# First scale row in two quarters of 256 columns; the first three up-projections over two of eight contraction tiles at once

## The chip, the cores and the metric

One core of one Trainium2 chip runs the whole layer as one program. The metric is the device time in microseconds (us) of one execution; a run gives several executions, and the median counts. A profiled execution also has a span, from its first to its last instruction, which is a little shorter than its device time.

## The reference, cut to what matters

The layer is a half-step gated feed-forward (SwiGLU), a pair of attention mixers, and a second half-step feed-forward. Only the way into the first feed-forward is touched:

```python
m = jnp.split((jax.nn.silu(c) @ w_ada[l] + b_ada[l])[:, None, :], N_MOD, axis=-1)     # 9 rows of 1024
x = _residual(x, _swiglu(_modnorm(x, g[0], m[0], m[1]), w1, w3, w2), g[1], m[2], HALF_STEP)
def _modnorm(x, g_pre, shift, scale):
    return _rmsnorm(x, g_pre) * (1 + scale) + shift
def _swiglu(h, w1, w3, w2):
    return (jax.nn.silu(h @ w1) * (h @ w3)) @ w2
```

`x` is 1024 tokens by 1024 channels, `w1` and `w3` are 1024 by 2816. So before the first product of a token with `w1` there must be the token's norm, and row `m[1]`, the scale, which is itself a product of `silu(c)` with 1024 columns of `w_ada`.

## The kernel before

Products in float32 quality are made of three in a faster format: each operand is split into a high part (ScalarE, a cast) and a low part (VectorE, the difference), and `mm3` adds high·high, high·low and low·high. The big products follow a Strassen scheme: tokens and channels are halved, and a `Unit` (line 500 on) is one tile of 128 output channels. Its `first` multiplies four contraction tiles of 128 channels (k = 0 to 3) of the first 512 tokens with the weight's quarter "11", 12 products of 128x512; its `second` does the same with k = 4 to 7 and "21".

At the head of the program four token tiles (`head`) are loaded, normalised (`normal`, line 910: a square with sum on ScalarE, two small operations on GpSimd, one multiplication on VectorE, in place), and turned by TensorE, so that channels lie on partitions. The turned tile k holds 512 tokens in one bank of PSUM. ScalarE then writes its high part, multiplied by the scale column `a0[:, 0, k]`, and VectorE its low part (`scaled_high`, line 974). ScalarE writes it once more in full (`scaled_all`). The shift row is added later, so the first four units (`RAW`) begin without it.

The scale row is made by `AdaHalf` (line 298), 512 columns at a time. For each of eight k it multiplies `sc[:, k, :]` (silu of c, padded to 32 columns) with 512 columns of `w_ada` in four groups of 128 columns; each group writes its own 32 partitions of one bank. `copy` brings the bank to SBUF, `turn` turns it into columns of 128, and adds the bias; `half_scale` makes `a0` from it. The first half (k = 0 to 3) is made here, two k after each token tile; the second half is made inside the plan.

Up to line 1000 the order of work is the order of the code, on each engine by itself: an engine takes its instructions strictly as they were written, and SyncE (SP) issues every load and store in one queue. From line 1060 a hand-written `Plan` sets the order: `step` lists the main work of TensorE, `side(i, ...)` what other work stands behind step i. Its first steps are `first` of units 0, 1, 2 (in two pieces, with k = 0 and k = 1 to 3) and the `second` of units 0 and 1. Behind step 0 stand the turning of k = 4 to 6, behind step 1 the products of the second row half (`row.step`), its copy and the turning of k = 7, behind step 2 the `half_scale(1)`, so that the row's `turn` comes between the two pieces of unit 2. The flag `units1[0].apart` makes unit 0 take all products that need a low part of the tokens last.

PSUM banks come from three rings, "s" and "m" with three banks, "v" with two; wide SBUF tiles for `w_ada` come from a pool of 16 (`V`).

## Time and profile before

| what | value |
|---|---|
| device time, three runs | 2557.73, 2560.17, 2561.82 us (median 2560.17) |
| device time of the profiled execution | 2559.68 us |
| its span | 2557.7 us |
| TensorE busy | 2527.3 us, 99% of the span |
| VectorE busy | 1936.3 us, 76% |
| ScalarE busy | 1259.2 us, 49% |
| mean of the clock granted to TensorE | 0.998 |
| first matrix instruction, first up-projection product | 9.90 us, 18.80 us |

In the rows of the timeline the columns are: start, length (both us), engine, line, operation, what it writes from what it reads, shape, number of instructions that the row merges, and in brackets the idle time of the engine before it and what ended it. Nearly all operations are recorded by a helper (line 120, 154 or 157), so the tiles' names tell what they are: `bs`, `bm`, `bv` are PSUM banks of the three rings, `sc` the silu of c, `ident` the matrix for turning, `a` the scale column. A row of windows gives, after the stretch and its length, the busy time and the number of instructions of TensorE, its weight loads, VectorE, ScalarE and GpSimd, and then the granted clock, the share of the DMA engines and GB/s. An instruction that reaches into a stretch counts in it.

### The profile page before, as it was taken

Reading aid. Unit: us, or ns where it says so; the run is one execution under the profiler, and the core shown is the slowest. Engines: PE = TensorE matmul, PEld = TensorE weight load, DVE = VectorE, ACT = ScalarE, POOL = GpSimd, SP = SyncE. Lnnn points to the kernel's source line nnn. Section 1 sums busy time; section 2 is a strip of 40 time slices with the busy share of each in tenths; the row PEclk is TensorE's granted clock in tenths of the full one; section 3 lists DMA queues with packets and bytes.
Section 4 is the critical chain, followed back from the end, with each engine's and each line's share of the span. In section 5 each row is a group of like instructions: output and inputs, shape, how many; then the busy total and the mean of one; then the engine's idle time right before and its main releaser. Section 6 shows DMA issues by size and latency. Waiting matters only on the chain. (4 is left out here: it accounts for less than half of the span.)

```text
span 2557.7 us, 38230 instructions
## 1 busy us (share of the span) xinstructions
PE 2527.3 (99%) x13416; PEld 2158.7 (84%) x13416; DVE 1936.3 (76%) x3629; ACT 1259.2 (49%) x2375; POOL 217.8 (9%) x372
## 2 busy tenths in 40 slices
PE   8999999999999999999999999999999999999998
PEld 6888888888998888889888999998888888888887
DVE  4789986887786577874568988887886888767777
ACT  5632223445654653433447987783266322233444
POOL 1000000001000000001003522221011000000003
PEclk9999999999999999999999999999999999999999
DMA  8455543943674666755978733207836445326724
GB/s 307 157 173 195 195 151 117 345 137 132 231 274 138 215 230 225 241 184 176 301 280 275 241 94 76 65 11 262 296 123 216 156 157 169 111 99 233 273 70 165
DMA packets 245760, 479.47 MB, mean 187 GB/s; under 512 B 30464, under 2 KB 71616, under 8 KB 245568
## 3 DMA queue, kind: packets, MB, share of 16 engines
q1 hardware_dynamic: 245568, 477.02, 55.4%
q8 instruction: 106, 1.74, 0.3%
q14 instruction: 86, 0.70, 0.1%
HBM read 348.93 MB, written 127.99 MB: 186 GB/s over the span
## 5 line engine op out<-in xcount | busy, mean ns | idle before, releaser
L120 ACT CAST xu<-t 128x512 fp32r<-128x512 f32 (+1 forms) x270 | 161.0, 601 | 494.4 <-DVE t L120 352.6
L154 PE MATMUL bm<-xu,xu 128*128 128x512 f32 (+2 forms) x1572 | 366.6, 386 | 0.0
L154 PE MATMUL bs<-xv,xu 128*128 128x512 f32 x1488 | 357.3, 389 | 0.3 <-DVE t L120 0.3
L154 PEld LDWEIGHTS bm<-xu,xu 128*128 128x128 f32 x1572 | 288.1, 188 | 56.7
L154 PE MATMUL bv<-xv,xu 128*128 128x512 f32 x1342 | 335.4, 389 | 0.0
L154 PEld LDWEIGHTS bs<-xv,xu 128*128 128x128 f32 x1488 | 279.1, 188 | 59.0 <-issue 1.1
L154 PEld LDWEIGHTS bv<-xv,xu 128*128 128x128 f32 x1342 | 251.8, 188 | 52.3
L154 PE MATMUL bs<-xv,xv 128*128 128x512 f32 x1086 | 265.8, 390 | 0.0
L120 DVE TENSOR_TENSOR xu<-xu,xu 128x512 fp32r<-128x512 f32 (+1 forms) x296 | 201.7, 686 | 55.2 <-ACT xu L120 54.9
L154 PEld LDWEIGHTS bs<-xv,xv 128*128 128x128 f32 x1086 | 203.0, 188 | 41.7
L154 PE MATMUL bs<-xu,xu 128*128 128x512 f32 (+1 forms) x972 | 226.2, 382 | 0.0
L120 DVE TENSOR_TENSOR t<-t,t 128x512 f32<-128x512 f32 (+2 forms) x278 | 185.1, 673 | 45.0 <-ACT t L120 36.0
L154 PE MATMUL bs<-w,w 96*128 96x512 f32 (+3 forms) x832 | 206.5, 367 | 4.7 <-DVE st L1802 4.0
L154 PEld LDWEIGHTS bs<-xu,xu 128*128 128x128 f32 x972 | 177.4, 188 | 35.7 <-issue 1.4
L120 POOL TENSOR_SCALAR st<-st 128x1 f32<-128x1 f32 (+1 forms) x66 | 33.5, 508 | 1887.4 <-ACT t L120 1869.2
L120 ACT CAST xv<-t 128x512 fp32r<-128x512 f32 x170 | 105.8, 622 | 169.8 <-PE bv L154 69.0
L120 DVE TENSOR_TENSOR xu<-t,xu 128x512 fp32r<-128x512 f32 (+1 forms) x270 | 179.0, 663 | 10.7 <-ACT xu L120 10.6
L154 PE MATMUL bm<-xv,xv 128*128 128x512 f32 x690 | 182.8, 390 | 0.0
L120 ACT CAST xu<-xu 128x512 fp32r<-128x512 f32 x218 | 132.7, 618 | 71.3 <-DMA xu<-in_wo 43.6
L120 DVE TENSOR_TENSOR xv<-t,xv 128x512 fp32r<-128x512 f32 x170 | 116.6, 686 | 65.6 <-ACT xv L120 56.5
L154 PE MATMUL bv<-t,w 128*128 128x256 f32 x896 | 150.9, 288 | 2.0 <-DVE t L1940 1.5
L154 PEld LDWEIGHTS bm<-xv,xv 128*128 128x128 f32 x690 | 129.2, 188 | 27.1 <-issue 0.4
(242 smaller groups left out, 4229.3 us busy)
## 6 DMA issues: line engine op xcount, KB each, us to landing
d<-t SPq DMA_DIRECT2D x366, 256.0 KB, 2.6
t<-d SPq DMA_DIRECT2D x274, 256.0 KB, 3.8
xu<-in_f1w SPq DMA_DIRECT2D x59, 512.0 KB, 4.2
xu<-in_f2w SPq DMA_DIRECT2D x58, 512.0 KB, 3.7
t<-in_wada SPq DMA_DIRECT2D x112, 256.0 KB, 5.1
xv<-in_f1w SPq DMA_DIRECT2D x44, 512.0 KB, 7.4
xu<-in_winT SPq DMA_DIRECT2D x38, 512.0 KB, 4.8
w<-d SPq DMA_DIRECT2D x32, 512.0 KB, 6.4
```

Of the source, the lines that this page charges most:

```text
L120: return lambda *x, **y: pin(f(*x, **y))
L154: return pin(nc.tensor.matmul(o, s, m, start=start, stop=stop, skip_group_check=open_group[0]))
```

## The change

The scale's first 512 columns become two quarters of 256 (`AdaQuarter`), each loaded by two transfers of 512 KB in place of four half-tiles' eight of 256 KB. A quarter uses two groups of 128 columns in place of four, and covers two contraction tiles. The first quarter stands ahead of the first up-projection weights in SP's queue, the second behind them. Each token tile is turned for k = 0, 1 only; the first quarter's products stand behind token tiles 1 and 2, its copy before the norm of token tile 3. Tiles k = 2, 3 are turned after that; `first` of units 0, 1 and 2 is called with k = 0, 1, with the second quarter between units 1 and 2, and the plan's main steps keep k = 2, 3 of them. The bank of turned tile 3 comes from ring "v" in place of "m".

```diff
+    class AdaQuarter(AdaHalf):
...
+        def load(self):
+            c = self.m * D + self.q * 256
+            for j in range(2):
+                t = V().rearrange("p (k c) -> p k c", k=4)
+                ld(t, a["wada"][j * 512:(j + 1) * 512, c:c + 256].rearrange("(k p) c -> p k c", p=P))
+                self.r += [t[:, k, :] for k in range(4)]
...
+        def step(self, ks):
+            if self.bank is None:
+                self.bank = PB("v")
+            for k in ks:
+                for g in range(2):
+                    mmul(self.bank[32 * g:32 * g + 32, :P], sc[:, k, :], self.r[k][:, g * P:(g + 1) * P],
+                         start=(k == 0), stop=(k == KD - 1))
...
+    quarters = [AdaQuarter(1, q) for q in range(2)]
...
-    h1rows[0][0].load()
+    quarters[0].load()
     for i in range(3):
         load_halves(i, 0)
+    quarters[1].load()
     h1rows[0][1].load()
...
-    first = [PB(t) for t in "sssm"]
+    first = [PB(t) for t in "sssv"]
     for i, x in enumerate(head):
         normal(x)
-        for k in range(4):
+        for k in range(2):
             turn_(first[k][:, i * P:(i + 1) * P], x[:, k * P:(k + 1) * P], ident)
-        h1rows[0][0].step(range(2 * i, 2 * i + 2))
-    h1rows[0][0].copy()
-    units1[0].split("11")
+        if i in (1, 2):
+            quarters[0].step(range(4 * i - 4, 4 * i))
+        if i == 2:
+            quarters[0].copy()
...
-    half_scale(0)
+    quarter_scale(0)
...
-    for k in range(4):
+    units1[0].cast("11")
+    for k in range(2):
         scaled_high(k, first[k])
+    units1[0].low("11")
+    for k in range(2, 4):
+        for i, x in enumerate(head):
+            turn_(first[k][:, i * P:(i + 1) * P], x[:, k * P:(k + 1) * P], ident)
     units1[1].split("11")
-    for k in range(4):
+    units1[0].first(Raw.f, range(0, 2))
+    units1[1].first(Raw.f, range(0, 2))
+    quarters[1].step(range(KD))
+    quarters[1].copy()
+    units1[2].split("11")
+    quarter_scale(1)
+    for k in range(2):
+        scaled_all(k, first[k])
+    for k in range(2, 4):
+        scaled_high(k, first[k])
+    units1[2].first(Raw.f, range(0, 2))
+    for k in range(2, 4):
         scaled_all(k, first[k])
...
-    go[2:3] = [lambda ks=ks: units1[2].first(Raw.f, ks) for ks in (range(0, 1), range(1, 4))]
+    go[:3] = [lambda u=u, ks=ks: u.first(Raw.f, ks) for u, ks in zip(units1[:3] + units1[2:3], [range(2, 4)] * 2 + [range(2, 3), range(3, 4)])]
```

VectorE at the head, before (rows in the engine's order; `xv_81` to `xv_84` are the four token tiles, `bv` the row's bank, `xu` the weights of a unit):

```order
L120 TENSOR_SCALAR xv_83<-xv_83,st_271 128x1024
L120 TENSOR_SCALAR xv_84<-xv_84,st_290 128x1024
L120 COPY t_306<-bv_240 128x128
L120 TENSOR_TENSOR xu_308<-xu_202,xu_308 128x512
L120 TENSOR_TENSOR mod_103<-bv_312,bada 128x4
L120 SCALAR_TENSOR_TENSOR a_311<-mod_103,ng 128x4
```

The same place with the change:

```order
L120 TENSOR_SCALAR xv_83<-xv_83,st_255 128x1024
L120 COPY t_269<-bv_243 64x128
L120 TENSOR_SCALAR xv_84<-xv_84,st_274 128x1024
L120 TENSOR_TENSOR mod_103<-bv_243,bada 128x2
L120 SCALAR_TENSOR_TENSOR a_280<-mod_103,ng 128x2
...
L120 SCALAR_TENSOR_TENSOR xv_294<-bs_221,a_280,xv_292 128x512
L120 SCALAR_TENSOR_TENSOR xv_294<-bs_222,a_280,xv_292 128x512
L120 TENSOR_TENSOR xu_290<-xu_194,xu_290 128x512
L120 TENSOR_TENSOR xu_309<-xu_196,xu_309 128x512
L120 COPY t_343<-bv_326 64x128
```

The copy of the row moved ahead of the norm of the last token tile (`xv_84`), and the low part of unit 0's weights (`xu_308` before, `xu_290` now) from ahead of the scale's sums to behind the low parts of two token tiles.

TensorE from unit 0's products on, with the change (`xv_292` and `xv_294` are the high and low parts of k = 0, 1; `xv_293` and `xv_295` those of k = 2, 3; `bm_312`, `bm_319`, `bm_359` the banks of units 0, 1, 2); before, all 12 products of unit 0 stood together behind one turning of the row:

```order
L154 MATMUL bm_312<-xv_292,xu_290 128x512
L154 MATMUL bm_312<-xv_294,xu_290 128x512
L154 MATMUL bm_312<-xv_292,xu_290 128x512 x2
...
L154 MATMUL bv_326<-xv_200,sc 32x128 x8
L154 MATMUL bv_326<-xv_202,sc 32x128 x8
L157 MATMUL bv_326<-ident,t_343 128x64
L154 MATMUL bm_359<-xv_292,xu_345 128x512
...
L154 MATMUL bm_312<-xv_293,xu_290 128x512 x4
L154 MATMUL bm_312<-xv_295,xu_290 128x512 x2
L157 MATMUL bs_424<-ident,xv_81 128x128
```

Unit 0's k = 0, 1 now go in plain `mm3` order, where the second product reads the tokens' low part and the third the weights' low part, since the call stands ahead of the line that sets `apart`.

TensorE around the turning of the second row half, before and then with the change (`t_486` and `t_496` are that row's copy, `xv_506` and `xv_515` the high parts of k = 4, 5):

```order
L154 MATMUL bm_496<-xv_322,xu_404 128x512
L157 MATMUL bv_500<-ident,t_486 128x128
L154 MATMUL bm_496<-xv_322,xu_404 128x512
L154 MATMUL bm_496<-xv_324,xu_404 128x512
...
L154 MATMUL bm_496<-xv_323,xu_404 128x512
L154 MATMUL bm_388<-xv_506,xu_422 128x512
```

```order
L154 MATMUL bm_359<-xv_293,xu_345 128x512
L157 MATMUL bv_509<-ident,t_496 128x128
L154 MATMUL bm_359<-xv_293,xu_345 128x512
L154 MATMUL bm_359<-xv_295,xu_345 128x512
L154 MATMUL bm_359<-xv_293,xu_345 128x512
L154 MATMUL bm_312<-xv_515,xu_439 128x512
```

Between the turning and the first product with k = 4 stood nine products of unit 2 before; three stand there now.

More of the change, by code (lines that the diff above doesn't have):

```diff
@@ L328, in turn, with __init__, copy @@
             b = slice(4 * self.h, 4 * self.h + 4)
+            for v in range(2):
+                vec.tensor_tensor(mod[self.m][:, v, b], pv[:, :, v], bada[:, self.m, b], op=ALU.add)
+                yield v
+    class AdaQuarter(AdaHalf):
+        def __init__(self, m, q):
+            self.m, self.q, self.r = m, q, []
+            self.bank = None
+        def load(self):
[11 more added lines that the diff above has]
+                         start=(k == 0), stop=(k == KD - 1))
+        def copy(self):
+            self.rows = T2()
+            vec.tensor_copy(self.rows[0:64, :P], self.bank[0:64, :P])
+        def turn(self):
+            pt = self.bank[:, 256:320]
+            turn_(pt, self.rows[0:64, :P], ident[0:64, 0:64])
+            pv = pt.rearrange("p (g c) -> p g c", c=32)
+            b = slice(2 * self.q, 2 * self.q + 2)
             for v in range(2):
@@ L943, in hybrid_block, with part_scale, quarter_scale @@
     units1[3].load(0)
-    first = [PB(t) for t in "sssm"]
+    first = [PB(t) for t in "sssv"]
     for i, x in enumerate(head):
         normal(x)
-        for k in range(4):
+        for k in range(2):
             turn_(first[k][:, i * P:(i + 1) * P], x[:, k * P:(k + 1) * P], ident)
-        h1rows[0][0].step(range(2 * i, 2 * i + 2))
-    h1rows[0][0].copy()
-    units1[0].split("11")
+        if i in (1, 2):
+            quarters[0].step(range(4 * i - 4, 4 * i))
+        if i == 2:
+            quarters[0].copy()
     banks[0] = "ss"
     a0 = const("a0", [P, 2, KD])
+    def part_scale(row, b):
+        for v in row.turn():
+            vec.scalar_tensor_tensor(a0[:, v, b], mod[1][:, v, b], 1.0, ng[:, 0, b], op0=ALU.add, op1=ALU.mult)
     def half_scale(h):
-        b = slice(4 * h, 4 * h + 4)
-        for v in h1rows[0][h].turn():
-            vec.scalar_tensor_tensor(a0[:, v, b], mod[1][:, v, b], 1.0, ng[:, 0, b], op0=ALU.add, op1=ALU.mult)
-    half_scale(0)
+        part_scale(h1rows[0][h], slice(4 * h, 4 * h + 4))
+    def quarter_scale(q):
+        part_scale(quarters[q], slice(2 * q, 2 * q + 2))
+    quarter_scale(0)
     class Raw:
@@ L1074, in hybrid_block @@
     row, sh = h1rows[0][1], h1rows[1]
-    side(0, lambda: units1[2].split("11"), *[lambda k=k: turn_k(k) for k in range(4, 7)],
+    side(0, *[lambda k=k: turn_k(k) for k in range(4, 7)],
          lambda: units1[0].split("21"), lambda: sh[0].load())
```

## The prediction

> **What bounds the kernel now.** I read the page first, then windows of the whole program, then the timeline of the head.

> ```profile
> PE 2527.3 (99%) x13416; PEld 2158.7 (84%) x13416; DVE 1936.3 (76%) x3629; ACT 1259.2 (49%) x2375; POOL 217.8 (9%) x372
> 35.70:100.00 64.30, 64.30 (x418) 53.19 (x418) 40.03 (x65) 44.69 (x78) 3.77 (x8) 1.00 0.58 196
> ```

> TensorE is busy 99% of the span, and from 35.70 us on (the last point that the change reorders) without a gap. What comes after is the same list on every engine, so a microsecond won or lost before 35.70 stays to the end. The question is when TensorE reaches that point, the products of the next row (the last row below).

> ```profile
> 9.90 0.90 PE L157 MATMUL bs<-ident,xv 128*128 128x128 f32 x3 [9.90 <-DVE xv L120]
> 10.56 0.75 DVE L120 TENSOR_SCALAR xv<-xv,st 128x1024 f32<-128x1024 f32 x1 [0.72 <-POOL st L120]
> 10.96 1.25 PE L154 MATMUL bv<-xv,sc 128*32 128x128 f32 x16
> 11.55 0.20 PEld L154 LDWEIGHTS bv<-xv,sc 128*32 128x32 f32 x8 [0.39 <-DMA xv<-in_wada]
> 12.03 0.75 DVE L120 TENSOR_SCALAR xv<-xv,st 128x1024 f32<-128x1024 f32 x1 [0.71 <-DMA xv<-in_wada]
> 13.50 0.76 DVE L120 TENSOR_SCALAR xv<-xv,st 128x1024 f32<-128x1024 f32 x1 [0.72 <-POOL st L120]
> 13.74 0.55 PE L157 MATMUL bs<-ident,xv 128*128 128x128 f32 x3
> 15.49 0.66 PE L154 MATMUL bv<-xv,sc 128*32 128x128 f32 x16
> 16.21 0.29 DVE L120 COPY t<-bv 128x128 f32<-128x128 f32 x1 [1.95 <-PE bv L154]
> 16.36 0.62 ACT L120 CAST xu<-xu 128x512 fp32r<-128x512 f32 x1 [5.10 <-DMA xu<-in_f1w]
> 16.56 0.33 PE L157 MATMUL bv<-ident,t 128*128 128x128 f32 x1 [0.41 <-DVE t L120]
> 17.01 0.69 DVE L120 TENSOR_TENSOR xu<-xu,xu 128x512 fp32r<-128x512 f32 x1 [0.51 <-ACT xu L120]
> 17.61 0.15 DVE L120 TENSOR_TENSOR mod<-bv,bada 128x4 f32<-128x4 f32 x1
> 18.07 1.84 ACT L120 ACTIVATE xv<-bs,a 128x512 fp32r<-128x512 f32 x3 [1.09 <-DVE mod L120]
> 18.78 2.07 DVE L120 SCALAR_TENSOR_TENSOR xv<-bs,a,xv 128x512 fp32r<-128x512 f32 x3 [0.55 <-ACT xv L120]
> 18.80 4.81 PE L154 MATMUL bm<-xv,xu 128*128 128x512 f32 x12 [1.92 <-ACT xv L120]
> 23.45 1.47 PE L157 MATMUL bs<-ident,xv 128*128 128x128 f32 x12
> 24.68 3.00 PE L154 MATMUL bm<-xv,xu 128*128 128x512 f32 x12
> 27.61 1.96 PE L154 MATMUL bv<-xv,sc 128*32 128x128 f32 x64
> 30.69 0.27 PE L157 MATMUL bv<-ident,t 128*128 128x128 f32 x1
> 30.71 5.05 PE L154 MATMUL bm<-xv,xu 128*128 128x512 f32 x21
> 31.45 1.85 ACT L120 ACTIVATE xv<-bs,a 128x512 fp32r<-128x512 f32 x3 [2.63 <-DVE mod L120]
> 32.17 2.07 DVE L120 SCALAR_TENSOR_TENSOR xv<-bs,a,xv 128x512 fp32r<-128x512 f32 x3 [0.55 <-ACT xv L120]
> 35.70 1.95 PE L154 MATMUL bv<-xv,sc 128*32 128x128 f32 x64
> ```

> The norms come every 1.47 us (10.56, 12.03, 13.50) and the row's data just as late. The row's copy starts at 16.21, its turning ends at 16.89, and TensorE then waits 1.92 us for the scale and the first high part. The first 12 products take 4.65 us to the next row (23.45), though 12 of unit 1 take 2.93 (24.68 to 27.61), 0.23 each and 0.2 for the switch to the row's products. The windows show why:

> ```profile
> 16.50:19.92 3.42, 1.44 (x5) 0.73 (x5) 2.29 (x8) 2.33 (x5) 0.00 (x0) 1.00 1.04 386
> 19.92:23.33 3.41, 3.41 (x9) 2.70 (x9) 2.19 (x4) 3.39 (x6) 0.00 (x0) 0.50 1.05 389
> ...
> 1351.12:1354.53 3.41, 1.21 (x7) 0.77 (x6) 1.79 (x9) 1.74 (x4) 0.00 (x0) 1.00 0.99 220
> 1354.53:1357.94 3.41, 3.41 (x17) 3.41 (x17) 2.98 (x13) 0.95 (x3) 0.00 (x0) 0.50 1.05 403
> 1757.30:1760.72 3.42, 1.84 (x8) 1.53 (x9) 2.49 (x5) 0.85 (x2) 0.00 (x0) 1.00 0.97 320
> ```

> The granted clock falls to 0.50 for 3.41 us after a stretch of the same length in which TensorE was busy 42% (1.44 of 3.42); the same happens after 35% at 1351, but the stretch at 1757 with 54% costs nothing.

> **The change, step by step**, on the clock of the profiled execution.

> *Row products.* A quarter has half the products of a half, but does it take half the time?

> ```profile
> 27.60:27.70 0.10, 0.10 (x5) 0.09 (x8) 0.00 (x0) 0.00 (x0) 0.00 (x0) 1.00 1.06 389
> 27.70:27.80 0.10, 0.10 (x8) 0.10 (x12) 0.00 (x0) 0.09 (x1) 0.00 (x0) 1.00 1.10 410
> 27.80:27.90 0.10, 0.10 (x12) 0.10 (x8) 0.00 (x0) 0.10 (x1) 0.00 (x0) 1.00 0.89 328
> ```

> Each count holds what is still in flight: 5, 8, 12, so four more each tenth. The four groups run side by side, a pass about every 0.11 us, and a product has two passes (64 records for 32). So eight k are 16 passes of 0.11, 1.96 us with the tail of the last. Two groups should run two at a time in the same 16 passes: a quarter would cost a half's 1.96, not 0.98. I take 1.96, since the row shows passes and not records setting the pace; 0.98 is the lower bound.

> *First quarter.* Transfers are served in order. The first two `wada` pieces, the bytes of the quarter's first transfer, are in at 11.55; the weights of unit 0, seven pieces later, at 16.36: 0.69 us for 256 KB. So the quarter's halves are in at 11.6 and 12.9, unit 0's weights at 13.6, the second quarter's two at 16.4 and 17.7. Token tile 1 is ready at 11.31 and turned twice by 11.85; passes begin at 11.95, at 0.21 each (TensorE is still at half speed: three turnings took 0.90 at 9.90, 0.55 at 13.74), then at 0.11, eight of them to 13.4. Token tile 2 (ready 12.78) is turned by 13.75, and the other eight passes end at 14.85. The copy follows at 14.9. **Behind it on VectorE waits the norm of token tile 3**, which ran at 13.50 before: now at 15.1 to 15.85, and TensorE waits for it. Turned at 16.0, the row's turning (no wait: its copy stands earlier on VectorE) at 16.2 to 16.5, the scale's first sum at 16.55. By the rows, the high part starts 0.46 behind that sum (18.07 less 17.61) and the first product 0.73 later (18.80 less 18.07): 17.7. Gain so far 1.1 us. The eight turnings for k = 2, 3 (0.9 us) lie in that wait and cost nothing; if the scale came earlier they would be the bound.

> *First products.* The second needs the first low part (0.75 from 17.7: 18.5). The third needs the low part of unit 0's weights, which VectorE now makes behind two low parts of 0.69: 17.7 + 3 x 0.69 = 19.75. Before, it was done at 17.70. From there ten products of 0.23 (four of unit 0, six of unit 1, whose weights are ready by 20.4) to 22.05. Casts on ScalarE are covered: it is free from 14.3.

> *Second quarter.* 1.96 from 22.15 to 24.1, copy to 24.4, turning at 24.5. Unit 2's six products begin behind it, to 26.05. On VectorE the low part of unit 2's weights (0.69) stands between copy and sums, so the sum comes at 24.9, the high part of k = 2 at 25.35, unit 0's rest at 26.1; its last product needs the low part of k = 3 (27.5) and the turnings of k = 4 start at 27.75. Before: 23.45. Later by 4.3, with 12 products done that came later before (2.75): **1.55 behind**.

> *Second row half.* Up to its turning, 30.69 less 23.45 is 7.24; six products fewer (1.38) leave 5.86: 33.6. From the turning the high part of k = 4 takes 0.76 to start (31.45 less 30.69) and the low part ends at 2.23 (32.17 plus 0.75, less 30.69). Nine products of unit 2 (2.07) covered that; three (0.69) don't. The second product with k = 4 starts 2.3 behind the turning, eleven products of 0.23 follow: 4.9 in all against 5.01 before, though six products (1.38) are gone. **Lost: 1.25.** The next row starts at 38.5 against 35.70: **2.8 us later**.

> *At nothing.* The next row's loads (four wide tiles, two of them freed by the second quarter at 24.1) are issued some tenths later, covered by the 38.5 at which they are needed; without that cover they would cost those tenths. Pieces of 1 KB in place of 2 KB have no row in the head; the nearest are stages with pieces of 512 B mostly, and of 2 KB:

> ```profile
> DMA packets 8390, 4.72 MB, mean 236 GB/s; under 512 B 577, under 2 KB 8390, under 8 KB 8390
> ...
> q1 hardware_dynamic: 8390, 4.72, 91.3%
> DMA packets 8098, 15.93 MB, mean 379 GB/s; under 512 B 1505, under 2 KB 1633, under 8 KB 8095
> ...
> q1 hardware_dynamic: 8095, 15.88, 102.1%
> ```

> Per share of the engines the short pieces move 70% as much (236/0.913 against 379/1.021). 1 KB lies between 70% and 100%; at 70% each quarter's transfer lands 0.6 late per 512 KB, and the copy about 0.4 late: +0.4 at most. I take 0.

> **Sum.** 2559.68 + 2.8 = 2562.5 for the profiled execution; it lies 0.5 below the median of the runs, so 2563.0.

> **Rivals.** *A quarter takes half the time* (0.98 by records). The first quarter then ends 0.9 sooner and the second is 1.0 shorter: +1.0, 2561.2. Against it: the four-at-a-time records.

> *The clock halves in the changed head too.* From 16.50 to 19.92 TensorE has 0.9 of turnings, two products of 0.39 and a part of the third, 1.8 of 3.42: 53%, between 42% (halved) and 54% (not). If it halves, 19.92 to 23.33 does half its work: +1.7, so +4.5, 2564.7. If the change escapes it, that gain stands in my 17.7 to 22.05 already.

> *Slower: the stretches lie elsewhere in the timed executions.* Place: the sparse time between 16.9 and 20. If before escapes its halved stretch there (4.65 less 2.76, with some 0.4 of waits that stay: 1.5 us won) and the change, whose sparse time is longer, does not, the distance is 2.8 + 1.5 + 1.7 = 6.0: 2566.2. It decides from stretches that start about 0.6 us later than in the profile, so that the 1.92 us gap is split between two. For it speaks that the three times lie 4.1 us apart; against it, that the profiled execution has the halved stretch and lies near their median.

> [...]

> *A gain over 0.2%* (5.1 us) is excluded nearly: all that the head could give back is the 1.92 of waiting and the 1.9 of half speed.

> **How the numbers follow.** Forecast 0.40, half-time quarters 0.15, halved clock 0.25, slower 0.18, anything else 0.02. The time is the likeliest's, 2563.0. The range runs from 1.7 below the half-time case to the slower one: 2559.5 to 2566.5; the likeliest alone has 2561.5 to 2564.5. About 0.2%, 5.1 us, is what a measurement of this kernel can tell from no change: slower by more is the slower case and a little of the halved clock, 0.21; within 0.77; faster 0.02.

> **What would show it.** First up-projection product near 17.7, third near 19.75, a norm of token tile 3 behind the copy near 15.1; the second quarter's products some 1.9 us long; an idle wait of about 0.7 us behind the turning of the second row half; the next row's start near 38.5 (40.1 with a window at 0.50 after 19.9). Wrong would be a quarter of about 1 us, or a next row before 36.5.

## The result, and the profile after

| | before | with the change |
|---|---|---|
| median, 12 runs each | 2560.03 us | 2563.84 us |
| lowest and highest | 2557.73 to 2561.82 | 2562.75 to 2568.23 |
| ratio, 95% interval | | 1.0016 (1.0009 to 1.0024) |
| profiled execution, its span | 2559.68, 2557.7 us | 2563.62, 2561.8 us |

The change costs 3.8 us by the medians, 0.15%. (The ratio with its interval is an estimate of its own from the runs; here and below it lies up to 0.0003 from the quotient of the medians.) The first part of the page of the changed kernel, and then a window from its next row's start on (the length, then the busy time of TensorE with its instructions, as in the rows shown of before):

```profile
PE 2529.0 (99%) x13417; PEld 2158.6 (84%) x13417; DVE 1937.7 (76%) x3634; ACT 1263.0 (49%) x2375; POOL 218.2 (9%) x372
```

```profile
40.14:100.00 59.86, 59.81 (x390) 49.14 (x390) 36.65 (x60) 41.68 (x73) 3.75 (x8) 1.00 0.55 181
```

From 40.14 us on TensorE is all but without a gap again (59.81 of 59.86 us), as it was from 35.70 in the profile of before: 4.44 later at the same point of the program. The timeline of the head, TensorE and VectorE:

```profile
11.21 0.75 DVE L120 TENSOR_SCALAR xv<-xv,st 128x1024 f32<-128x1024 f32 x1 [0.72 <-POOL st L120]
11.68 1.92 PE L154 MATMUL bv<-xv,sc 128*32 128x128 f32 x16 [0.45 <-DMA xv<-in_wada]
13.54 0.69 PE L157 MATMUL bs<-ident,xv 128*128 128x128 f32 x2
14.15 1.86 PE L154 MATMUL bv<-xv,sc 128*32 128x128 f32 x16
16.07 0.28 DVE L120 COPY t<-bv 64x128 f32<-64x128 f32 x1 [4.10 <-PE bv L154]
16.27 0.73 DVE L120 TENSOR_SCALAR xv<-xv,st 128x1024 f32<-128x1024 f32 x1
17.06 0.44 PE L157 MATMUL bs<-ident,xv 128*128 128x128 f32 x2 [1.05 <-DVE xv L120]
18.94 0.49 PE L154 MATMUL bm<-xv,xu 128*128 128x512 f32 x1 [0.21 <-ACT xv L120]
19.73 0.50 PE L154 MATMUL bm<-xv,xu 128*128 128x512 f32 x1 [0.29 <-DVE xv L120]
20.99 2.56 PE L154 MATMUL bm<-xv,xu 128*128 128x512 f32 x10 [0.76 <-DVE xu L120]
23.48 1.94 PE L154 MATMUL bv<-xv,sc 128*32 128x128 f32 x32
25.81 0.27 PE L157 MATMUL bv<-ident,t 64*128 64x64 f32 x1 [0.39 <-DVE t L120]
29.24 1.47 PE L157 MATMUL bs<-ident,xv 128*128 128x128 f32 x12
35.10 0.27 PE L157 MATMUL bv<-ident,t 128*128 128x128 f32 x1
36.61 0.50 PE L154 MATMUL bm<-xv,xu 128*128 128x512 f32 x1 [0.54 <-ACT xv L120]
37.39 2.82 PE L154 MATMUL bm<-xv,xu 128*128 128x512 f32 x11 [0.28 <-DVE xv L120]
40.14 1.95 PE L154 MATMUL bv<-xv,sc 128*32 128x128 f32 x64
```

The copy of the row (16.07) stands ahead of the last token tile's norm (16.27); VectorE had been idle for 4.10 us before it, though the norm could have run (it does so at 12.67 in the first experiment below). The two halves of the first quarter take 1.92 and 1.86 us. The first of the early products starts at 18.94, 0.14 later than the first product did before (18.80). The second quarter has half the products of a row half, x32 in place of x64, and takes as long: 1.94 against 1.95 us.

The windows of the same kernel (the last three columns are granted clock, DMA share, GB/s; the trace has the clock at full from 15.82 on):

```profile
8.99:12.41 3.42, 2.10 (x12) 1.34 (x14) 1.53 (x3) 1.76 (x4) 3.00 (x6) 1.00 1.09 362
12.41:15.82 3.41, 3.41 (x30) 2.33 (x26) 0.00 (x0) 0.62 (x1) 0.23 (x1) 1.00 1.07 364
15.82:19.23 3.41, 2.15 (x16) 1.39 (x12) 1.80 (x7) 1.03 (x2) 0.00 (x0) 1.00 1.07 374
19.23:22.65 3.42, 2.37 (x9) 1.59 (x9) 2.30 (x4) 2.44 (x5) 0.00 (x0) 1.00 1.05 386
```

Until 15.82 TensorE ran at half speed, as the durations show: two turnings took 0.69 us at 13.54 and 0.44 at 17.06 (the column of the clock says 1.00 ahead of its first event, and cannot be used there). Afterwards no stretch of the head is halved; the sparse ones are busy 63% and 69%.

How the distance to before runs through the program, by the start of the same instruction of VectorE, counted from the end of its list, against the first profile of before (us; worked out from the traces):

| | at 100 | at 1345 | at 1380 | at 2300 |
|---|---|---|---|---|
| the change | +4.57 | +4.51 | +3.01 | +3.85 |
| the change, second profile | +3.88 | +3.82 | +1.98 | +2.59 |
| before, second profile | -2.31 | -2.35 | -2.80 | -2.93 |

So in the profiles the loss is all made in the head. Some 1.5 to 1.8 of it disappear near 1350, where the first profile of before has a halved stretch (0.50 from 1354.53 to 1357.94) and the first of the change has none.

### The profile page after: what moved, and what is told of

The parts are those of the page before. It is cut to its first block, busy times and chain, and to the rows that moved or that the text cites. A ratio compares the mean times of both kernels' runs of the same rounds, so it can differ in the third digit from the quotient of the medians.

```text
span 2561.8 us, 38238 instructions
## 1 busy us (share of the span) xinstructions
PE 2529.0 (99%) x13417; PEld 2158.6 (84%) x13417; DVE 1937.7 (76%) x3634; ACT 1263.0 (49%) x2375; POOL 218.2 (9%) x372
## 3 DMA queue, kind: packets, MB, share of 16 engines
q8 instruction: 106, 1.74, 0.3%
## 5 line engine op out<-in xcount | busy, mean ns | idle before, releaser
L120 ACT CAST xu<-t 128x512 fp32r<-128x512 f32 (+1 forms) x270 | 161.4, 603 | 494.4 <-DVE t L120 352.0
L154 PE MATMUL bm<-xu,xu 128*128 128x512 f32 (+2 forms) x1572 | 366.6, 387 | 0.0
L154 PE MATMUL bs<-xv,xu 128*128 128x512 f32 x1488 | 357.3, 389 | 0.3 <-DVE t L120 0.3
L154 PEld LDWEIGHTS bm<-xu,xu 128*128 128x128 f32 x1572 | 288.0, 188 | 56.7 <-ACT t L120 0.2
L154 PE MATMUL bv<-xv,xu 128*128 128x512 f32 x1342 | 335.5, 389 | 0.0
L154 PEld LDWEIGHTS bs<-xv,xu 128*128 128x128 f32 x1488 | 279.1, 188 | 59.0 <-issue 1.1
L154 PEld LDWEIGHTS bv<-xv,xu 128*128 128x128 f32 x1342 | 251.8, 188 | 52.3
L154 PE MATMUL bs<-xv,xv 128*128 128x512 f32 x1086 | 265.8, 390 | 0.0
L120 DVE TENSOR_TENSOR xu<-xu,xu 128x512 fp32r<-128x512 f32 (+1 forms) x296 | 202.2, 688 | 53.8 <-ACT xu L120 53.4
L154 PEld LDWEIGHTS bs<-xv,xv 128*128 128x128 f32 x1086 | 203.0, 188 | 41.7
L154 PE MATMUL bs<-xu,xu 128*128 128x512 f32 (+1 forms) x972 | 226.2, 382 | 0.0
L120 DVE TENSOR_TENSOR t<-t,t 128x512 f32<-128x512 f32 (+2 forms) x278 | 185.4, 674 | 45.1 <-ACT t L120 36.2
L154 PE MATMUL bs<-w,w 96*128 96x512 f32 (+3 forms) x832 | 206.2, 366 | 4.7 <-DVE st L1861 4.4
L154 PEld LDWEIGHTS bs<-xu,xu 128*128 128x128 f32 x972 | 177.4, 188 | 35.7 <-issue 1.4
L120 POOL TENSOR_SCALAR st<-st 128x1 f32<-128x1 f32 (+1 forms) x66 | 33.5, 508 | 1892.0 <-ACT t L120 1873.7
L120 ACT CAST xv<-t 128x512 fp32r<-128x512 f32 x170 | 106.1, 624 | 169.5 <-PE bv L154 69.0
L120 DVE TENSOR_TENSOR xu<-t,xu 128x512 fp32r<-128x512 f32 (+1 forms) x270 | 179.5, 665 | 10.7 <-ACT xu L120 10.6
L154 PE MATMUL bm<-xv,xv 128*128 128x512 f32 x690 | 182.9, 390 | 0.0
L120 ACT CAST xu<-xu 128x512 fp32r<-128x512 f32 x218 | 133.1, 620 | 69.9 <-DMA xu<-in_wo 55.4
L120 DVE TENSOR_TENSOR xv<-t,xv 128x512 fp32r<-128x512 f32 x170 | 117.2, 690 | 64.8 <-ACT xv L120 55.9
L154 PE MATMUL bv<-t,w 128*128 128x256 f32 x896 | 150.8, 288 | 2.3 <-DVE t L1999 1.7
L154 PEld LDWEIGHTS bm<-xv,xv 128*128 128x128 f32 x690 | 129.2, 188 | 27.1 <-issue 0.4
```

What stands on the lines that cost most here:

```text
L120: return lambda *x, **y: pin(f(*x, **y))
L154: return pin(nc.tensor.matmul(o, s, m, start=start, stop=stop, skip_group_check=open_group[0]))
```

## The experiments

Each is the changed kernel with one edit, unless it says otherwise; the difference of medians is to the kernel before on the same chip (2559.55, then 2559.3, then 2558.58 us), and the next row's start is that of the products with which the row shown at 40.14 begins.

| run | next row | norm of token tile 0 to next row | first product to next row | median less before | ratio, 95% interval |
|---|---|---|---|---|---|
| before | 35.70 | 26.61 | 16.90 | | |
| before, second profile | 33.56 | 25.51 | 15.52 | | |
| the change | 40.14 | 31.88 | 21.20 | +3.81 | 1.0016 (1.0009 to 1.0024) |
| the change, second profile | 39.19 | 31.14 | 21.14 | | |
| copy behind the norm | 38.64 | 30.39 | 21.21 | +3.63 | 1.0016 (1.0006 to 1.0025) |
| unit 0's low part early | 38.77 | 30.60 | 20.19 | +3.24 | 1.0014 (1.0004 to 1.0023) |
| quarter over four groups | 38.19 | 29.94 | 20.52 | +4.63 | 1.0019 (1.0009 to 1.0028) |
| cover behind the row's turning | 38.17 | 30.15 | 19.83 | +3.39 | 1.0014 (1.0005 to 1.0023) |
| first, second and fourth together | 37.00 | 28.79 | 18.84 | +1.81 | 1.0005 (0.9996 to 1.0014) |
| all four | 35.01 | 26.76 | 18.18 | -0.06 | 0.9998 (0.9990 to 1.0007) |
| spare turnings ahead of the quarter | 40.20 | 32.09 | 21.18 | +3.06 | 1.0015 (1.0006 to 1.0024) |
| before, spare turnings in its gap | 34.36 | 26.23 | 15.51 | -0.62 | 0.9997 (0.9988 to 1.0006) |
| before, only the products split | 38.00 | 29.85 | 18.49 | +0.21 | 1.0001 (0.9992 to 1.0010) |
| quarters, products whole | 38.96 | 30.63 | 15.67 | +3.13 | 1.0011 (1.0002 to 1.0020) |

The second column of numbers takes out when the head's data came: token tile 0's norm starts at 9.09 us in the first profile of before and at 8.02 to 8.33 in the thirteen others. The third begins at the first up-projection product, so when the clock first rose doesn't enter it, with one exception: in the kernel with the quarter over four groups it begins at half speed. In the first profile of before and in the kernel with only the products split it holds a stretch at 0.50. It repeats well, 21.20, 21.14, 21.21 and 21.18 where nothing behind the first product was edited, and is the cleaner measure of what stands there.

**The copy behind the last norm.**

```diff
-        if i == 2:
-            quarters[0].copy()
+    quarters[0].copy()
```

> The copy of the first quarter goes behind the norm of the last token tile on VectorE. In the changed kernel the next row's products start at 40.1 us. Theory (the late steps add up, each is worth what it shows): the last norm starts at 12.7 in place of 16.3, the turning of the quarter comes 1.0 us sooner and the next row starts at 39.1. Rival (what is late hides behind something else that is late, above all the clock at half speed until 15.8): the start moves by less than 0.3. With the clock at full speed from 12.4 on, both come another 1.6 sooner.

VectorE and then TensorE in this kernel's timeline:

```profile
12.67 0.75 DVE L120 TENSOR_SCALAR xv<-xv,st 128x1024 f32<-128x1024 f32 x1 [0.72 <-POOL st L120]
15.59 0.28 DVE L120 COPY t<-bv 64x128 f32<-64x128 f32 x1 [2.17 <-PE bv L154]
```

```profile
14.02 1.52 PE L154 MATMUL bv<-xv,sc 128*32 128x128 f32 x16
17.43 0.49 PE L154 MATMUL bm<-xv,xu 128*128 128x512 f32 x1 [0.21 <-ACT xv L120]
```

The norm runs 3.6 us earlier, at once behind its input, and the next row starts 1.50 earlier than in the change's first profile, of which some 0.3 is an earlier clock (the second eight passes took 1.52 in place of 1.86), and 0.55 earlier than in its second. From the end of the second eight passes to the first product, a stretch at full clock in all three profiles, it takes 2.93 us in both profiles of the change (16.01 to 18.94, 15.12 to 18.05) and 1.89 here (15.54 to 17.43). So the wait lies on the path and is worth 1.04; the medians, 0.2 apart on other chips, cannot show it.

**The low part of unit 0's weights early**, ahead of the scale.

```diff
+    units1[0].split("11")
     quarter_scale(0)
...
-    units1[0].cast("11")
...
-    units1[0].low("11")
```

> The low part of unit 0's weights is made before the scale's sums, as in the kernel before. Theory: the third up-projection product no longer waits (0.76 us of idle time before it gone, and the wait for the tokens' low parts alone is left), next row at 39.1 against 40.1. Rival: less than 0.3.

TensorE behind the first product:

```profile
19.37 2.83 PE L154 MATMUL bm<-xv,xu 128*128 128x512 f32 x11 [0.28 <-DVE xv L120]
```

The wait of 0.76 ahead of the third product is gone: behind a wait of 0.28 for the tokens' low part 11 products follow without a gap, and the next row starts at 38.77, 20.19 behind the first product where the change has 21.20 and 21.14. That is the 1.0 of the theory; in the medians (0.6) it is again less than their intervals.

**The quarter over four column groups**: odd k go to the other two groups, and their sums are added when the bias is.

```diff
-                    mmul(self.bank[32 * g:32 * g + 32, :P], sc[:, k, :], self.r[k][:, g * P:(g + 1) * P],
-                         start=(k == 0), stop=(k == KD - 1))
+                    o = 64 * (k % 2) + 32 * g
+                    mmul(self.bank[o:o + 32, :P], sc[:, k, :], self.r[k][:, g * P:(g + 1) * P],
+                         start=(k < 2), stop=(k >= KD - 2))
...
-                vec.tensor_tensor(mod[self.m][:, v, b], pv[:, :, v], bada[:, self.m, b], op=ALU.add)
+                vec.tensor_tensor(mod[self.m][:, v, b], pv[:, 0:2, v], bada[:, self.m, b], op=ALU.add)
+                vec.tensor_tensor(mod[self.m][:, v, b], pv[:, 2:4, v], mod[self.m][:, v, b], op=ALU.add)
```

> Odd contraction slices of a quarter go to the other two column groups, so four groups run side by side again; two small additions on VectorE sum the two halves. If passes set the pace, a quarter falls from 1.94 us to about 0.98 at full speed (3.8 to 1.9 at half speed), and the next row starts at about 38.2 against 40.1. If products set the pace, a quarter stays at 1.9 and the small additions cost 0.2 to 0.4.

TensorE in this kernel's timeline, and a window:

```profile
11.56 1.08 PE L154 MATMUL bv<-xv,sc 128*32 128x128 f32 x16 [0.34 <-DMA xv<-in_wada]
22.20 1.08 PE L154 MATMUL bv<-xv,sc 128*32 128x128 f32 x32
```

```profile
12.67:16.08 3.41, 2.34 (x22) 1.52 (x23) 0.95 (x2) 0.62 (x1) 0.00 (x0) 1.00 1.07 363
16.08:19.50 3.42, 3.18 (x11) 2.05 (x9) 2.71 (x9) 2.57 (x5) 0.00 (x0) 1.00 1.06 377
```

The same 32 products take 1.08 us over four groups in place of 1.94 over two, so passes set the time here. But the median did not move down (+4.6 against +3.8, a difference well inside the intervals). The profile shows one thing that can work against it: the shorter first quarter leaves a gap in the stretch from 12.67 to 16.08 (busy 69%), and the clock rises only at 19.50. The profiled execution, 2561.25, is the lowest of this kernel's ten, so what the others did is not seen.

**Cover behind the turning of the second row half**: its products one step earlier, and six products of unit 2 behind its turning.

```diff
-    go[:3] = [... zip(units1[:3] + units1[2:3], [range(2, 4)] * 2 + [range(2, 3), range(3, 4)])]
+    go[:3] = [... zip((units1[0], units1[1], units1[1], units1[2]), (range(2, 4), range(2, 3), range(3, 4), range(2, 4)))]
...
-         lambda: units1[0].split("21"), lambda: sh[0].load())
-    side(1, lambda: row.step(range(KD)), row.copy, lambda: turn_k(7), lambda: units1[1].split("21"))
-    side(2, lambda: half_scale(1), *[lambda k=k: scaled_high(k, turned[k]) for k in range(4, KD)])
+         lambda: units1[0].split("21"), lambda: sh[0].load(),
+         lambda: row.step(range(KD)), row.copy, lambda: turn_k(7), lambda: units1[1].split("21"))
+    side(1, lambda: half_scale(1), *[lambda k=k: scaled_high(k, turned[k]) for k in range(4, KD)])
```

> The second row half comes before the rest of unit 1, its turning behind the first half of that rest, so nine products stand between the turning and the first product with k = 4, as in the kernel before. Theory: the two waits of 0.54 and 0.28 us behind the turning go, next row at 38.9 against 40.1. Rival (the wait is at the tokens' low parts wherever the turning stands): less than 0.3.

TensorE behind the row's turning:

```profile
33.10 0.27 PE L157 MATMUL bv<-ident,t 128*128 128x128 f32 x1
33.13 5.12 PE L154 MATMUL bm<-xv,xu 128*128 128x512 f32 x21
38.17 1.95 PE L154 MATMUL bv<-xv,sc 128*32 128x128 f32 x64
```

The waits of 0.54 and 0.28 behind the turning are gone, and from the turning to the next row 21 products stand in 5.07 us, where 15 stood in 5.04. The head is 1.4 us shorter, from token tile 0's norm (30.15 against 31.88 and 31.14) as from the first product (19.83 against 21.20 and 21.14).

**All four together.**

> All four edits together: copy behind the last norm, unit 0's weights' low part before the sums, four groups side by side, nine products of cover. Theory (the steps add, less what two of them share): next row at 34.9 us, 5.2 sooner than in the changed kernel and 0.8 sooner than in the kernel before, time about 2559.3. Rival (the split into two quarters costs by itself, whatever the order): not before 37, time over 2561.

TensorE:

```profile
11.80 1.08 PE L154 MATMUL bv<-xv,sc 128*32 128x128 f32 x16 [0.59 <-DMA xv<-in_wada]
17.62 2.83 PE L154 MATMUL bm<-xv,xu 128*128 128x512 f32 x11 [0.28 <-DVE xv L120]
20.38 1.08 PE L154 MATMUL bv<-xv,sc 128*32 128x128 f32 x32
35.01 1.96 PE L154 MATMUL bv<-xv,sc 128*32 128x128 f32 x64
```

The whole loss is gone, to within an interval of -2.6 to +1.8 us, and nothing is won on before; the rival, a next row not before 37, is out. The four shortenings of the head add up to 5.0 singly (31.5, the mean of the change's two profiles, less each), and together they gave 4.7.

**The three edits of order without the fourth.**

> The three edits of order together, with the narrow quarters as the change has them. Theory (the losses lie one behind the other, so they add): the next row starts at 36.5 us where the change has 40.1 and all four edits had 35.0, and the median lies 1 to 2 us above that of the kernel before, between the change (+3.8) and all four edits (-0.1). Rival (only the shorter passes let the others count): the median stays at +3 or above.

The next row starts at 37.00 and the median lies 1.8 above before, with an interval that holds no change: by the medians about half of the loss is order, and the rest of it needs the shorter passes. In the heads, 2.7 of the 31.5 us from norm to next row go by order and 2.0 more by the passes. The order's losses add as the theory had it: behind the first product the low part gave 1.0 and the cover 1.3, and the three edits together give 2.3 there (18.84; the copy's edit works ahead of it). In the medians the fourth edit did nothing by itself and 1.9 on top of the three. That fits the gap that it left alone: with all four the stretch ahead of the clock's rise is filled by the norm's earlier turnings (busy 3.42 of 3.42 us from 12.61), and it rose at 16.03 instead of 19.50. It is an explanation that fits and not one that is shown, since the profile of the fourth edit alone is of its fastest execution.

**Spare turnings ahead of the quarter**, seven whose results nobody reads, to bring the clock up sooner.

```diff
+        if i == 0:
+            spare = PB("m")
+        for k in range((4, 3, 0, 0)[i]):
+            turn_(spare[:, k * P:(k + 1) * P], x[:, k * P:(k + 1) * P], ident)
```

> The changed kernel with seven more turnings of the first two token tiles into a bank that nobody reads, in TensorE's idle time before the first quarter's products. If the clock rises when TensorE was busy enough in the stretch before, it rises at the end of the stretch that holds the token tiles, one stretch (3.4 us) sooner than 15.8, and the next row starts at 38.6 against 40.1 with a median 1 to 1.5 us lower. If it rises at a fixed time after the start of the work, nothing changes, or up to 0.4 us are lost on the added turnings.

Its windows:

```profile
8.53:11.95 3.42, 2.80 (x11) 2.07 (x11) 1.84 (x3) 2.30 (x4) 1.90 (x5) 1.00 1.08 371
11.95:15.36 3.41, 3.08 (x24) 2.33 (x26) 0.00 (x0) 0.62 (x1) 0.55 (x1) 1.00 1.07 366
```

A miss: the stretch that they fill is busy 82%, and the clock still rises only behind the next one, at 15.36. The first quarter's passes began at 12.28, later than with the change. The test says nothing on what an earlier clock would be worth. Nor does it speak for a rise at a fixed time: over the 14 profiles TensorE's first instruction starts between 8.8 and 9.9 us, and the clock rises between 13.09 and 21.19.

**Before, with its gap filled**: 12 spare turnings behind the scale's first row half, read by nobody.

```diff
     half_scale(0)
+    spare = PB("m")
+    for x in head[:3]:
+        for k in range(4):
+            turn_(spare[:, k * P:(k + 1) * P], x[:, k * P:(k + 1) * P], ident)
```

> The kernel before with twelve turnings into a bank that nobody reads, in the 1.9 us in which TensorE waits for the scale. If it is that idle time that halves the clock from 19.9 to 23.3, the stretch at 0.50 goes, the next row starts at 34.2 in place of 35.7 and the time falls by up to 1.5 us. If it is something else, the stretch stays and the start is within 0.2 of 35.7.

Two windows of it, the second of which ends with the clock's rise:

```profile
8.47:11.88 3.41, 2.54 (x21) 1.40 (x22) 1.92 (x3) 1.93 (x4) 3.06 (x5) 1.00 1.05 388
11.88:15.30 3.42, 3.42 (x36) 2.32 (x39) 0.76 (x1) 0.00 (x0) 0.55 (x1) 1.00 1.02 373
```

No halved stretch, the first 12 products in 3.39 in place of 4.81, the next row at 34.36, near the 34.2 foreseen. The median is 0.6 lower, and the interval holds no change. The kernel before without filling had no halved stretch in its second profile either, so the filling only insures against something that comes by chance. Up to the scale TensorE's order here is that of the kernel before, and yet the clock rises only at 15.30; the first of the two windows was busy 74%.

**Before, with only the products split**: the first row half stays whole, units 0 to 2 take k = 0, 1 early.

```diff
-    for k in range(4):
+    for k in range(2):
         scaled_high(k, first[k])
     units1[1].split("11")
+    units1[0].first(Raw.f, range(0, 2))
+    units1[1].first(Raw.f, range(0, 2))
+    units1[2].split("11")
     for k in range(2, 4):
         scaled_high(k, first[k])
+    units1[2].first(Raw.f, range(0, 2))
...
-    go[2:3] = [lambda ks=ks: units1[2].first(Raw.f, ks) for ks in (range(0, 1), range(1, 4))]
+    go[:3] = [... zip(units1[:3] + units1[2:3], [range(2, 4)] * 2 + [range(2, 3), range(3, 4)])]
...
```

> The kernel before (one half of 512 columns, no quarters) with only the up-projections of units 0 to 2 over k = 0, 1 first. Theory: the split by itself costs the lost cover behind the second row half's turning and gains a few tenths of waiting for the low parts of k = 2, 3: next row at 36.7 against 35.7; the rest of the change's cost is the quarters'. Rival (the split is what costs): 38 or later.

Windows of this kernel:

```profile
9.86:13.28 3.42, 2.98 (x34) 1.67 (x36) 1.99 (x3) 0.87 (x2) 2.42 (x4) 1.00 1.05 385
13.28:16.69 3.41, 3.41 (x36) 2.11 (x28) 0.04 (x1) 0.62 (x1) 0.00 (x0) 1.00 1.05 388
16.69:20.10 3.41, 1.59 (x20) 0.70 (x18) 1.97 (x7) 1.33 (x3) 0.00 (x0) 1.00 1.04 385
20.10:23.52 3.42, 3.23 (x8) 2.55 (x9) 3.32 (x6) 3.42 (x7) 0.00 (x0) 0.50 1.06 391
```

The median is that of before, +0.2, but its interval, -2.0 to +2.6 us, holds the theory's 1.0 as well as the rival's 2.3. The next row at 38.00 is what the rival gave. Part of that is the clock: it is at full only from 16.69, and still at half speed behind the stretch that ends at 13.28, busy 87%; the first product starts 0.71 later than in the first profile of before. The rest is the split: from the first product on both of these profiles hold one halved stretch, and it takes 18.49 here against 16.90. That is 1.6 more, with waits of 0.54 and 0.29 behind the second row half's turning as in the change. Behind the head the profiled execution made the 2.3 good: its span is 2557.4 us, that of before 2557.7. A next row read from one profile is uncertain by some 2 us, as the two profiles of before show.

**Quarters with whole products.**

```diff
-    units1[0].first(Raw.f, range(0, 2))
-    units1[1].first(Raw.f, range(0, 2))
     quarters[1].step(range(KD))
     quarters[1].copy()
-    units1[2].split("11")
     quarter_scale(1)
...
-    units1[2].first(Raw.f, range(0, 2))
...
-    go[:3] = [... zip(units1[:3] + units1[2:3], [range(2, 4)] * 2 + [range(2, 3), range(3, 4)])]
+    go[2:3] = [lambda ks=ks: units1[2].first(Raw.f, ks) for ks in (range(0, 1), range(1, 4))]
...
```

> The scale row in two quarters, but the up-projections over four contraction tiles as before: both quarters ahead of the first product. Theory (the quarters cost, and the early products only give part of it back): the second quarter runs from 18.9, when its transfer and the turnings are done, to 20.9, the first product starts at 23.0 to 24.0 us and the next row at 40 to 42 us; the median lies 3 to 6 us above the kernel before. Rival (the early products are the cost, not the quarters): within 1.5 us of the kernel before.

TensorE in this kernel's timeline:

```profile
20.37 2.31 PE L154 MATMUL bv<-xv,sc 128*32 128x128 f32 x32
23.29 3.53 PE L154 MATMUL bm<-xv,xu 128*128 128x512 f32 x12
38.96 1.95 PE L154 MATMUL bv<-xv,sc 128*32 128x128 f32 x64
```

Here the first product comes 4.35 us later than in the changed kernel, and still its next row is 1.2 and 0.2 us earlier than in the change's two profiles; the median is +3.1 against +3.8. So the quarters cost, as the theory had it (with a second quarter that came later than foreseen, at 20.37, with the clock still at half speed until 21.19), but its other half fell: the early products, as the change places them, give nothing back that can be seen. This kernel is also without the two losses that they bring, the late low part (12 products follow without a gap) and the thin cover (nine products stand behind the row's turning again): from the first product on it takes 15.67, as before does without a halved stretch (15.52 and 15.51).

**Both kernels a second time**, unchanged.

> The changed kernel unchanged, for a second profile. Theory (the late rise of the clock belongs to the changed head, since its gaps between turnings keep the first stretch from filling): full speed again later than 14.5 us, and the next row at 39 to 41 us. Rival (it was one execution's chance): full speed near 13.1 us and the next row at 38.5.

> The kernel before unchanged, for a second profile. Theory (its first profile had its head's data 0.9 us late and its clock early, which about cancel): the norm of token tile 0 at 8.0 to 8.3 us, full speed between 13 and 17 us, the next row at 35 to 38 us. Rival (the first profile is typical): full speed at 13.1 us, the next row at 35.7.

The change's second profile, TensorE:

```profile
11.28 1.92 PE L154 MATMUL bv<-xv,sc 128*32 128x128 f32 x16 [0.26 <-DMA xv<-in_wada]
13.75 1.37 PE L154 MATMUL bv<-xv,sc 128*32 128x128 f32 x16
18.05 0.50 PE L154 MATMUL bm<-xv,xu 128*128 128x512 f32 x1 [0.21 <-ACT xv L120]
39.19 1.96 PE L154 MATMUL bv<-xv,sc 128*32 128x128 f32 x64
```

Two windows of the second profile of before, the one that ends with the clock's rise and the sparse one behind it:

```profile
9.96:13.37 3.41, 3.10 (x37) 1.74 (x36) 1.89 (x3) 0.53 (x2) 1.81 (x3) 1.00 1.05 383
16.78:20.20 3.42, 2.16 (x8) 1.28 (x9) 2.80 (x9) 2.90 (x6) 0.00 (x0) 1.00 1.05 388
```

With the clock at full from 14.41, a tenth short of what the theory gave and far from the rival's 13.1, the change's first product starts at 18.05 and the next row at 39.19. Before reaches its next row at 33.56, ahead of the 35 to 38 foreseen: its data came early, the clock rose at 13.37, and the sparse stretch, busy 63% this time, was not followed by a halved one.

## Why the prediction was right, and where it was off

*Direction, mechanism and range* held: 2563.0 forecast, 2563.84 measured, within 0.2% of before and above it. That the time came so near is in part luck: in the profile the head lost 1.6 us more than forecast, and 1.5 came back near 1350, where the forecast had nothing.

*Row products.* Right, and shown: a quarter over two groups costs 1.94 us, and the same products over four groups 1.08. The rival of the half-time quarter is out.

*Transfers.* Right: the quarter's data are in at 11.68 (11.6 forecast) and the passes begin with them, where the forecast had token tile 1 as the later of the two, at 11.95; unit 0's cast starts at 13.74 (13.6). The bound of +0.4 for pieces of 1 KB was not needed: behind the first quarter no matrix instruction of the head waits for a transfer.

*First quarter.* This is the step that was mis-sized. It set passes "at 0.21 each", "then at 0.11, eight of them to 13.4", with full speed at the 13.09 of the profile of before. Full speed came at 15.82 and 14.41 in the change's two profiles, so the two halves took 1.92 and 1.86 (1.92 and 1.37) in place of 1.45 and 1.1, and the first product started at 18.94 (18.05) in place of 17.7: 1.24 (0.35) late. The clock had been carried over as a time; in each of the 14 profiles it rose behind a stretch of 3.41 us in which TensorE was busy 3.08 us or more. Before keeps TensorE busy from 9.90 on in its first profile and from 10.29 in its second; in the change two turnings per token tile leave it idle until the quarter's data are in, at 11.3 to 11.7. So with the change such a stretch can begin to fill 1 to 1.8 us later, by these times. But 13.09 was also the earliest of several: TensorE's order ahead of the scale is the same in the two kernels made from before, and there the clock rose at 15.30 and 16.69. With the change's order ahead of the first product it rose at 14.41, 14.79 (the kernel with cover) and 15.82, and only at 21.19 with the products whole. How much of the 1.24 is the order and how much the chance of where the stretches lie stays open.

*First products, second quarter, second row half.* Right within 0.4: from the first product to the next row 20.8 us were forecast, 21.20 and 21.14 measured. The third product came 2.05 behind the first, as forecast; the wait behind the row's turning was 0.54 and 0.28 (about 0.7 forecast). The copy's place, the weights' late low part and the thin cover are each shown by the edit that undoes it: the wait goes from the timeline, and some 1.0, 1.0 and 1.3 us with it. None of the three is shown by its median.

*The sum.* 2.8 forecast for the profiled execution, 3.94 measured: 4.44 in the head (2.8, the 1.24 of the clock, and 0.4 of small pieces), 1.5 back near 1350, some 0.8 more lost by 2300, for which nothing here gives a cause. The forecast that everything behind the head stays as it is was thus not exact; the part near 1350 lies where the two programs are the same.

*Rivals.* The change's head had no halved stretch in either profile: its sparse stretches were busy 63% and 69%. Of the slower rival one half happened, before escaping its halved stretch, in the second profile: the heads then lie 5.6 us apart (39.19 less 33.56). But that execution, 2556.75, is faster than all 21 others of before on its chip, the lowest of which took 2557.47. The medians lie 3.8 apart, between the forecast's 2.8 and the 5.6; how often the stretch is halved is not known from two profiles of each.

What stays open: why the single edits moved the medians by 0.2 to 0.6 (and one by -0.8) when their heads became 0.9 to 1.6 shorter, while all four together gave 3.9 and 4.7. The intervals, some 2 us to each side, are wide enough to hold it. The four profiled executions do follow their heads: they took 2562.26, 2561.85, 2561.25 and 2561.54 where the change's two took 2563.62 and 2562.35, so 0.7 to 1.7 less than the mean of these. But each is among the three fastest of its kernel's ten, and what the heads of the other executions looked like is not known.

## What to carry to other kernels

The row of narrow products, whose four column groups run side by side, was paid by passes: 32 products on two of the four groups took 1.94 us, 64 on all four 1.95, so two quarters cost two halves, and a second copy, turning and scale. When work is cut finer to start earlier, look at what stood behind each moved piece on its engine, here a norm behind a copy and a low part behind two others: each of these cost about a microsecond. Do not carry a clock's rise over from an old trace as a time; work out from the new order when TensorE is first busy without gaps, and allow for chance besides: one and the same order of TensorE's work gave rises from 13.09 to 16.69 here.

## What the runs showed of the hardware that was not expected

```profile
1344.57:1347.98 3.41, 1.82 (x12) 1.26 (x10) 2.67 (x10) 0.89 (x2) 0.00 (x0) 1.00 0.54 176
1754.17:1757.58 3.41, 1.75 (x8) 1.28 (x8) 2.76 (x5) 0.52 (x1) 0.00 (x0) 1.00 1.00 294
```

53% was halved and 51% was not, so the busy share alone doesn't decide there, and the cases are those of this program and no threshold. Near 1350, with no edit anywhere near, the first profile of before has the halved stretch of 3.41 us and the first of the change has none: between 1345 and 1380 the change gains 1.5 us on before.
